# Order of products, buffers of raw strips and staging of gated blocks in a SwiGLU layer

## The chip, the cores and the metric

The kernel runs on one core of a Trainium2 chip. The metric is the device time of one execution in microseconds (us). The core's engines are TensorE (PE, matmuls), VectorE (DVE), ScalarE (ACT), GpSimd (POOL) and SyncE (SP); SP issues most DMA transfers, and each engine works through its own queue of instructions in order.

## What is computed

One decoder layer for a prompt of 1024 rows and 8 x 4 sample rows, 1056 columns T of activations in all. The change touches the last third of it, the SwiGLU feed-forward block:

```python
x = layer_norm(DEEPNORM_ALPHA * x + memory_attention(x, mem_k, mem_v, w_mem_q, w_mem_o), ln2_g, ln2_b)
ffn = (jax.nn.silu(x @ w_gate) * (x @ w_up)) @ w_down
x = layer_norm(DEEPNORM_ALPHA * x + ffn, ln3_g, ln3_b)
```

Here x has 1024 features and D_FF is 2816, which is NF = 22 strips of 128 hidden features. Inputs are float32.

## The kernel before

**Tiles.** The 1056 columns are three blocks, BLK: block 0 and block 1 of 384 columns, block 2 of 288. A float32 product is made of three reduced-precision (fp32r) matmuls: high times high, high times low, low times high (mm3, lines L209 to L211, and the function product). So each operand is first split: ScalarE casts the high part, VectorE subtracts it from the raw value and keeps the low part. Names that end in h or begin with whi are high parts; l and wlo mark low parts. (A weight unit of gate_up is one tile [128, 2, 512] with both parts, under the tag whi or wlo.)

**Stages.** gate_up_first makes strips f = 0 and 1 (NC = 2) with plain products (gemm). Its evacuation applies Silu on ScalarE (L948), multiplies on VectorE (L951) and writes the gated block sil to the DRAM scratch s_h (put, L938, on SP's queue). In the same stage combine makes the sums of activation blocks that gate_up needs: sums sq on GpSimd and VectorE (L973), casts (L979), low parts x1l, x6l, x7l on VectorE (L980).

gate_up makes f = 2 to 21. A pair f is a gate strip and an up strip of 1024 weights, four quarters a11, a12 (gate) and a21, a22 (up). Blocks 0 and 1 are computed by seven products instead of eight, as Strassen's scheme does: m4 and m3 use a22 and a11 alone, m2, m5, m1, m6, m7 use sums of quarters. Each is 12 matmuls of 384 columns. Block 2 takes four plain products (a11, a12, a21, a22), 48 matmuls of 288 columns, and these stand last in a pair. The nine units of a pair are made in the order of `names`: GpSimd sums quarters into wt (L1011, 3 buffers), ScalarE casts (L1013), VectorE subtracts (L1014). The code makes units four ahead of the product at hand; the scheduler then puts each engine's instructions in an order by its own planning, fixed when the kernel is built.

**Raw strips.** raw(f) loads the two strips of a pair on SP's queue (L994): the gate strip into tag wraw of the long-lived pool w, the up strip into tag wru of the pool up, two buffers each. The pool up (wru, wt and the products' staging) lies where the pool ln3 lay, which holds the sil and sq tiles of gate_up_first, so the first loads into wru and the first wt wait until those are done with.

**down** goes over the hidden strips in five groups (DOWN: 4, 4, 4, 2, 8 strips). For each block of a group it loads the gated strips from s_h, four at a time (hr, L1100), casts (L1103) and subtracts (L1104), and multiplies with the strips of w_down: each weight strip gives two outputs of four 128-row steps, block 0 for eight outputs, then block 1, then block 2. s_h is one DRAM tile, so a load from it waits for every write to it that stands earlier in the program.

Of the kernel before, what the change touches and what calls it, by code (L numbers as in the profile page):

```python
# [10 lines left out]
F32R = mybir.dt.float32r  # L11
# [11 lines left out]
NF = 22  # L23
# [117 lines left out]
class Body:  # L141
# [121 lines left out]
    def phase12(self, st):  # L263
# [13 lines left out]
        self.s_x1 = scr("s_x1", [128, 8 * T])  # L277
        self.s_h = scr("s_h", [128, NF * T])
        self.qs = self.t(self.cp, [128, 4, 32], "qs")
# [614 lines left out]
    def rest(self):  # L894
        tc, nc, a = self.tc, self.nc, self.a
        v, act, g, mm = nc.vector, nc.scalar, nc.gpsimd, nc.tensor.matmul
        x = self.x
        xs = lambda b, k: tuple(t_[:, k % 4, :] for t_ in x[b][k // 4])
        with tc.tile_pool(name="mq", bufs=1) as qp:
            self.mem_attention(qp, x, xs)  # L900
        with tc.tile_pool(name="z2", bufs=1) as zp:
            z = self.load_z(zp, self.s_x1)
            with tc.tile_pool(name="xc", bufs=1) as xp:
                with tc.tile_pool(name="ln3", bufs=1) as self.lp:
                    self.mem_out(z, xp, x, xs)
                    X = self.gate_up_first(z, xp, x, xs)
                with tc.tile_pool(name="up", bufs=1) as up:
                    self.gate_up(up, X, x[2])
            with tc.tile_pool(name="ln4", bufs=1) as self.lp, tc.tile_pool(name="ffn", bufs=1) as fp:
                self.down(z, fp)  # L910
# [25 lines left out]
    def put(self, t_, f, b):  # L936
        off, n = BLK[b]
        self.nc.sync.dma_start(self.s_h[:, NF * off + f * n:NF * off + (f + 1) * n], t_[:, :n])  # L938


    def gate_up_first(self, z, xp, x, xs):
        nc, sil, X = self.nc, {}, {}

        def evac(s, b, ps):
# [19 lines left out]
    def combine(self, X, xp, z, names):  # L964
# [5 lines left out]
        for n in names:  # L970
# [11 lines left out]
            yield  # L982

    def gate_up(self, up, X, x2):
        tc, nc, a = self.tc, self.nc, self.a
        v, act, g = nc.vector, nc.scalar, nc.gpsimd
        raws, units = {}, {}

        def raw(f):
            if f >= NF:  # L990
                return
            raws[f] = [self.t(self.wp, [128, 1024], "wraw", bufs=2), self.t(up, [128, 1024], "wru", bufs=2)]
            for i, r in enumerate(raws[f]):
                nc.sync.dma_start(r[:], a["wst"][GU + 2 * f + i])  # L994


        names = ("a22", "a11", "m2", "m5", "m1", "m6", "m7", "a12", "a21")

        def unit(i):
            f, n = NC + i // 9, names[i % 9]  # L1000
            if f >= NF:
                return
            if n == "a22":
                raw(f + 1)
            q = {f"a{1 + j // 2}{1 + j % 2}": raws[f][j // 2][:, 512 * (j % 2):512 * (j % 2) + 512] for j in range(4)}
            src = q.get(n)
            if src is None:
                p_, q_, op = {"m2": ("a21", "a22", OP.add), "m5": ("a11", "a12", OP.add), "m1": ("a11", "a22", OP.add),
                              "m6": ("a21", "a11", OP.subtract), "m7": ("a12", "a22", OP.subtract)}[n]
                src = self.t(up, [128, 512], "wt", bufs=3)[:]  # L1010
                g.tensor_tensor(out=src, in0=q[p_], in1=q[q_], op=op)  # L1011
# [14 lines left out]
        tt = v.tensor_tensor  # L1026
        raw(NC)
        for i in range(4):
            unit(i)
        at = 4  # L1030
        for f in range(NC, NF):
            U = lambda n: units[f, n]

            def step():
                nonlocal at
                unit(at)
                at += 1

            p4, p3 = self.ps(), self.ps()
            e4, e3, e1, d, s2 = (tmp(n, c) for n, c in (("e4", 1), ("e3", 2), ("e1", 2), ("ed", 1), ("s2", 2)))  # L1040
# [29 lines left out]
            step()  # L1070
            n = BLK[2][1]
            pg, pu = self.ps2(), self.ps2()
            product(pg, n, U("a11"), *x2[0])
            product(pg, n, U("a12"), *x2[1], first=False)
            sil = tmp("sil", 1)
            act.activation(sil[:, :n], pg[:, :n], AF.Silu)
            step()
            product(pu, n, U("a21"), *x2[0])
            product(pu, n, U("a22"), *x2[1], first=False)
            tt(out=sil[:, :n], in0=sil[:, :n], in1=pu[:, :n], op=OP.mult)  # L1080
            self.put(sil, f, 2)
            step()


    def down(self, z, fp):
# [3 lines left out]
        for ci, (f0, nf) in enumerate(DOWN):  # L1089
# [5 lines left out]
            for b, (off, n) in enumerate(BLK):  # L1095
                H[b] = []
                for k0 in range(0, nf, 4):
                    nk = min(4, nf - k0)
                    r = self.t(fp, [128, 4, 384], "hr")[:, :nk, :n]
                    nc.sync.dma_start(r, self.s_h[:, NF * off + (f0 + k0) * n:NF * off + (f0 + k0 + nk) * n]  # L1100
                                      .rearrange("p (k n) -> p k n", n=n))
                    h, l = (self.t(self.ap_, [128, 4, n], f"a{(ci + k0 // 4) % 2}{p}{b}", F32R)[:, :nk] for p in "hl")
                    nc.scalar.copy(h, r)  # L1103
                    nc.vector.tensor_tensor(out=l, in0=r, in1=h, op=OP.subtract)  # L1104
                    H[b].append((h, l))

# [401 lines left out]
```

## Time and profile before

| | us |
|---|---|
| runs | 1733.98, 1729.49, 1733.06 |
| median | 1733.06 |
| the profiled execution | 1729.63 |
| its span | 1727.8 |
| TensorE busy in the span | 1612.6 |
| VectorE, ScalarE, GpSimd busy | 937.8, 593.3, 553.3 |

The profile is that of one execution. The page gives busy time by engine and the chain of work that ended last; a chain row has a start, a length and what ran or was waited for. A table of windows gives, for a stretch, the busy time and number of instructions of each engine, the clock granted to TensorE as a share of 2.4 GHz, the busy share of the DMA engines and GB/s. A list of waits names the waiting engine and line, then what ended the wait, total us, times and longest us. A group of instructions has its count, busy time and mean ns, then the idle time ahead of it. gate_up_first ends at about 1004 us of the span, gate_up at 1436.4, down follows.

### The profile page before, as it was taken

How to read it: one execution, taken by the hardware profiler on the slowest of the kernel's cores; microseconds unless marked ns; L12 is line 12 of the kernel's file. 1: busy time of each engine (PE TensorE's matmuls, PEld its weight loads, DVE VectorE, ACT ScalarE, POOL GpSimd, SP SyncE). 2: the span in 40 equal slices, each digit the busy share in tenths (PEclk: the TensorE clock that was granted, in tenths of full speed). 3: DMA queues.
4: the chain of work that ended last, by engine and by line, in shares of the span. 5: the costliest groups of instructions: out<-in, count | busy, mean ns of one | idle time of the engine just before them, and what ended most of it. 6: DMA issues, size and time to landing. Idle time of an engine off the chain costs nothing.

```text
span 1727.8 us, 27767 instructions
## 1 busy us (share of the span) xinstructions
PE 1612.6 (93%) x10910; PEld 1472.8 (85%) x10910; DVE 937.8 (54%) x1754; ACT 593.3 (34%) x1149; POOL 553.3 (32%) x534
## 2 busy tenths in 40 slices
PE   7898898999999988999998979999999997999996
PEld 7787785666776978987798979999999997999995
DVE  7555482077545986235527765555555544544645
ACT  5211121186334255235404633333333332211312
POOL 3404402042222644002126555455554440000033
PEclk9998999999999998999999989999999998999998
DMA  7535776813422356126621212222222214422301
GB/s 271 119 67 144 203 202 174 273 67 126 139 70 85 127 196 223 49 84 213 243 74 46 67 66 75 78 75 78 75 75 75 75 62 142 141 83 68 113 38 64
DMA packets 103779, 200.71 MB, mean 116 GB/s; under 512 B 14240, under 2 KB 60832, under 8 KB 102880
## 3 DMA queue, kind: packets, MB, share of 16 engines
q1 hardware_dynamic: 90976, 152.79, 28.3%
q10 hardware_dynamic: 12672, 46.14, 8.0%
q8 instruction: 86, 1.41, 0.3%
q14 instruction: 45, 0.37, 0.1%
HBM read 153.85 MB, written 45.04 MB: 115 GB/s over the span
## 4 chain that ended last, share of the span: by engine, by line
PE 74%; DVE 11%; DMA 7%; ACT 2%; issue 2%; POOL 2%; SPq 1%; ACTq 0%; POOLq 0%; DVEq 0%
PE g L1021 16%; PE g L209 12%; PE g L211 12%; PE g L210 12%; PE s L1021 7%; PE s L575 2%; DMA wraw<-in_wst_dram 2%; PE s L577 2%; DVE wlo L191 1%; PE g L599 1%; DMA skv<-in_ckT_dram 1%; PE q L750 1%; POOL z L831 1%; DMA skv<-in_cv_dram 1%; PE g L411 1%
## 5 line engine op out<-in xcount | busy, mean ns | idle before, releaser
L209 PE MATMUL g<-a0h,whi 128*128 128x384 f32 (+1 forms) x768 | 255.9, 335 | 21.7 <-ACT a0h L1103 11.7
L211 PE MATMUL g<-a0h,wlo 128*128 128x384 f32 (+1 forms) x768 | 252.8, 329 | 5.0 <-DVE wlo L191 5.0
L210 PE MATMUL g<-a0l,whi 128*128 128x384 f32 (+1 forms) x768 | 253.9, 331 | 0.1
L209 PE MATMUL g<-a1h,whi 128*128 128x384 f32 (+1 forms) x672 | 221.4, 330 | 0.8 <-ACT a1h L335 0.8
L210 PE MATMUL g<-a1l,whi 128*128 128x384 f32 (+1 forms) x672 | 218.2, 325 | 2.9 <-DVE a1l L337 1.8
L211 PE MATMUL g<-a1h,wlo 128*128 128x384 f32 (+1 forms) x672 | 218.9, 326 | 0.0
L209 PEld LDWEIGHTS g<-a0h,whi 128*128 128x128 f32 x768 | 148.4, 194 | 27.8 <-ACT a0h L1103 12.0
L211 PEld LDWEIGHTS g<-a0h,wlo 128*128 128x128 f32 x768 | 148.7, 194 | 7.2 <-DVE wlo L191 5.7
L190 ACT CAST whi<-wraw 128x1024 fp32r<-128x1024 f32 x84 | 88.0, 1049 | 185.1 <-PE g L210 116.6
L210 PEld LDWEIGHTS g<-a0l,whi 128*128 128x128 f32 x768 | 148.9, 194 | 2.1 <-DVE a0l L1104 0.7
L191 DVE TENSOR_TENSOR wlo<-wraw,whi 128x1024 fp32r<-128x1024 f32 x84 | 113.3, 1352 | 68.2 <-ACT whi L190 67.9
L209 PEld LDWEIGHTS g<-a1h,whi 128*128 128x128 f32 x672 | 128.3, 191 | 6.0 <-issue 3.1
L210 PEld LDWEIGHTS g<-a1l,whi 128*128 128x128 f32 x672 | 128.2, 191 | 4.1 <-DVE a1l L337 2.0
L211 PEld LDWEIGHTS g<-a1h,wlo 128*128 128x128 f32 x672 | 128.0, 191 | 1.3 <-issue 1.1
L1011 POOL TENSOR_TENSOR wt<-wraw,wru 128x512 f32<-128x512 f32 x40 | 52.6, 1315 | 136.5 <-DVE wlo L1014 136.5
L776 DVE TENSOR_TENSOR z<-z,g 128x384 f32<-128x384 f32 (+1 forms) x96 | 49.1, 518 | 86.2 <-PE g L211 86.2
L1013 ACT CAST wlo<-wt 128x512 fp32r<-128x512 f32 x100 | 60.2, 618 | 83.4 <-PE g L1021 74.0
L1014 DVE TENSOR_TENSOR wlo<-wt,wlo 128x512 fp32r<-128x512 f32 x100 | 83.1, 846 | 3.0 <-ACT wlo L1013 1.4
L784 POOL TENSOR_TENSOR acc<-z 128x384 f32<-128x384 f32 (+1 forms) x6 | 8.0, 1339 | 205.4 <-DVE z L776 191.7
L1049 DVE TENSOR_TENSOR ed<-e,g 128x384 f32<-128x384 f32 x20 | 11.1, 554 | 105.9 <-PE g L1021 102.5
L831 POOL TENSOR_SCALAR z<-z,vneg,vecs 128x384 f32<-128x384 f32 (+1 forms) x36 | 50.5, 1414 | 43.6 <-DVE z L827 43.6
L587 POOL TENSOR_SCALAR S<-S,rD 128x128 f32<-128x128 f32 (+7 forms) x64 | 38.5, 607 | 68.7 <-DVE rD L586 49.8
(457 smaller groups left out, 4033.8 us busy)
## 6 DMA issues: line engine op xcount, KB each, us to landing
wraw<-in_wst_dram ACTq DMA_DIRECT2D x88, 512.0 KB, 3.9
skv<-in_ckT_dram SPq DMA_DIRECT2D x40, 256.0 KB, 4.6
skv<-in_cv_dram SPq DMA_DIRECT2D x40, 256.0 KB, 4.6
wraw<-in_wst_dram SPq DMA_DIRECT2D x20, 512.0 KB, 3.7
wru<-in_wst_dram SPq DMA_DIRECT2D x20, 512.0 KB, 4.4
kvm<-in_cmk_dram SPq DMA_DIRECT2D x16, 512.0 KB, 4.9
wraw<-in_cmv_dram SPq DMA_DIRECT2D x16, 512.0 KB, 4.1
hr<-s_h SPq DMA_DIRECT2D x10, 768.0 KB, 4.2
```

The costliest lines, as they stand in the source:

```text
L190: self.nc.scalar.copy(h[:], r[:])
L191: self.nc.vector.tensor_tensor(out=l[:], in0=r[:], in1=h[:], op=OP.subtract)
L209: mm(out, wh, xh, start=start, stop=False)
L210: mm(out, wh, xl, start=False, stop=False)
L211: mm(out, wl, xh, start=False, stop=stop)
L587: g.tensor_scalar(out=S[:, :w], in0=S[:, :w], scalar1=rD[:], scalar2=1.0, op0=OP.mult, op1=OP.mult)
L776: self.nc.vector.tensor_tensor(out=z[:, k], in0=z[:, k], in1=ps[:, :n], op=OP.add)
L831: g.tensor_scalar(out=z[:, k], in0=z[:, k], scalar1=sc, scalar2=bi, op0=OP.mult, op1=OP.add)
L1011: g.tensor_tensor(out=src, in0=q[p_], in1=q[q_], op=op)
L1013: act.copy(t_[:, 0], src)
L1014: v.tensor_tensor(out=t_[:, 1], in0=src, in1=t_[:, 0], op=OP.subtract)
L1021: nc.tensor.matmul(ps[:, :n], p_, q_, start=first and k + j == 0, stop=k == 3 and j == 2, skip_group_check=not first)
```

## The change

- raw(f) becomes a method; both strips of a pair go to one tag, wraw for even f, wru for odd f, two buffers each. raw(2) is called in gate_up_first, behind the write of strip 1's block 0, instead of at the start of gate_up; raw(f + 1) goes with the first unit of f.
- The four products of block 2 come first in each pair, and the units are made in the order a11, a12, a21, a22, m2, m5, m1, m6, m7. wt has two buffers.
- The scratch s_h becomes 33 tiles, one for two strips of one block.
- down loads two strips at a time into tiles of half the size. For the first group all six loads go through one tile hr0 that is allocated ahead of gate_up_first, for the others through two buffers.

```diff
-        self.s_h = scr("s_h", [128, NF * T])
+        self.s_h = {(f, b): scr(f"s_h{f}_{b}", [128, 2 * BLK[b][1]]) for f in range(NF // 2) for b in range(3)}
...
             z = self.load_z(zp, self.s_x1)
+            self.hr = self.t(zp, [128, 2, 384], "hr0")
...
     def put(self, t_, f, b):
-        off, n = BLK[b]
-        self.nc.sync.dma_start(self.s_h[:, NF * off + f * n:NF * off + (f + 1) * n], t_[:, :n])
+        n = BLK[b][1]
+        self.nc.sync.dma_start(self.s_h[f // 2, b][:, f % 2 * n:(f % 2 + 1) * n], t_[:, :n])
...
             self.put(sil[b], s // 2, b)
+            if s == 2 * NC - 1 and b == 0:
+                self.raw(NC)
...
+    def raw(self, f):
+        if f >= NF:
+            return
+        pool, tag = ((self.wp, "wraw"), (getattr(self, "up", None), "wru"))[(f - NC) % 2]
+        self.raws[f] = [self.t(pool, [128, 1024], tag, bufs=2) for _ in range(2)]
+        for i, r in enumerate(self.raws[f]):
+            self.nc.sync.dma_start(r[:], self.a["wst"][GU + 2 * f + i])
...
-        def raw(f):
-            if f >= NF:
-                return
-            raws[f] = [self.t(self.wp, [128, 1024], "wraw", bufs=2), self.t(up, [128, 1024], "wru", bufs=2)]
...
-        names = ("a22", "a11", "m2", "m5", "m1", "m6", "m7", "a12", "a21")
+        names = ("a11", "a12", "a21", "a22", "m2", "m5", "m1", "m6", "m7")
...
-            if n == "a22":
-                raw(f + 1)
+            if n == names[0]:
+                self.raw(f + 1)
...
-                src = self.t(up, [128, 512], "wt", bufs=3)[:]
+                src = self.t(up, [128, 512], "wt", bufs=2)[:]
...
-        raw(NC)
...
+            n = BLK[2][1]
+            pg, pu = self.ps2(), self.ps2()
+            product(pg, n, U("a11"), *x2[0])
+            product(pg, n, U("a12"), *x2[1], first=False)
...
+            product(pu, n, U("a21"), *x2[0])
+            product(pu, n, U("a22"), *x2[1], first=False)
...
-                for k0 in range(0, nf, 4):
-                    nk = min(4, nf - k0)
-                    r = self.t(fp, [128, 4, 384], "hr")[:, :nk, :n]
-                    nc.sync.dma_start(r, self.s_h[:, NF * off + (f0 + k0) * n:NF * off + (f0 + k0 + nk) * n]
-                                      .rearrange("p (k n) -> p k n", n=n))
...
+                for k in range(0, nf, 2):
+                    r = (self.hr if not ci else self.t(fp, [128, 2, 384], "hr", bufs=2))[:, :, :n]
+                    nc.sync.dma_start(r, self.s_h[(f0 + k) // 2, b][:].rearrange("p (k n) -> p k n", n=n))
```

**Entry of gate_up, SP's queue.** From the first raw load to the first load into wru, before (wraw_10114 and wru_10115 are the gate and up strip of f = 2, wraw_10118 and wru_10119 those of f = 3):

```order
L994 DMA wraw_10114<-in_wst_dram 128x1024
L994 DMA wraw_10118<-in_wst_dram 128x1024
L938 DMA s_h<-sil_9745 128x384
L938 DMA s_h<-sil_9828 128x384
L938 DMA s_h<-sil_9889 128x384
L938 DMA s_h<-sil_9943 128x384
L938 DMA s_h<-sil_10005 128x288
L938 DMA s_h<-sil_10077 128x288
L994 DMA wru_10115<-in_wst_dram 128x1024
L994 DMA wru_10119<-in_wst_dram 128x1024
```

And now (wraw_9897 and 9898 are both strips of f = 2, wru those of f = 3; s_h_0_97, s_h_1_98 and s_h_2_99 are blocks 0, 1, 2 of strips 0 and 1):

```order
L995 DMA wraw_9897<-in_wst_dram 128x1024
L995 DMA wraw_9898<-in_wst_dram 128x1024
L939 DMA s_h_0_97<-sil_9778 128x384
L939 DMA s_h_0_97<-sil_9861 128x384
L1104 DMA hr_1671_8946<-s_h_0_97 128x768
L939 DMA s_h_1_98<-sil_9926 128x384
L939 DMA s_h_1_98<-sil_9980 128x384
L939 DMA s_h_2_99<-sil_10042 128x288
L939 DMA s_h_2_99<-sil_10114 128x288
L995 DMA wru_10151<-in_wst_dram 128x1024
L995 DMA wru_10152<-in_wst_dram 128x1024
```

The second load ahead of the writes belongs to f = 2 instead of f = 3, both loads behind the last write belong to f = 3, and a load of hr0 stands behind the second write of block 0.

**Entry of gate_up, VectorE.** From the low part x1l to the first subtraction for a unit of gate_up, before (whi_10122 is a22 of f = 2):

```order
L980 TENSOR_TENSOR x1l_10014<-sq_10011,x1h_10013 128x1536
L951 TENSOR_TENSOR sil_10005<-sil_10005,g_10017 128x288
L980 TENSOR_TENSOR x6l_10047<-sq_10044,x6h_10046 128x1536
L980 TENSOR_TENSOR x7l_10080<-sq_10050,x7h_10079 128x1536
L951 TENSOR_TENSOR sil_10077<-sil_10077,g_10083 128x288
L1014 TENSOR_TENSOR whi_10122<-wru_10115,whi_10122 128x512
```

And now (whi_10155, wlo_10158, whi_10164, wlo_10161 are a11, a12, a22, a21 of f = 2):

```order
L984 TENSOR_TENSOR x1l_10051<-sq_10048,x1h_10050 128x1536
L1020 TENSOR_TENSOR whi_10155<-wraw_9897,whi_10155 128x512
L1020 TENSOR_TENSOR wlo_10158<-wraw_9897,wlo_10158 128x512
L953 TENSOR_TENSOR sil_10042<-sil_10042,g_10054 128x288
L984 TENSOR_TENSOR x6l_10084<-sq_10081,x6h_10083 128x1536
L1020 TENSOR_TENSOR whi_10164<-wraw_9898,whi_10164 128x512
L1020 TENSOR_TENSOR wlo_10161<-wraw_9898,wlo_10161 128x512
L984 TENSOR_TENSOR x7l_10117<-sq_10087,x7h_10116 128x1536
L953 TENSOR_TENSOR sil_10114<-sil_10114,g_10120 128x288
```

Four subtractions of f = 2 (L1020, L1014 before) stand ahead of the last product sil, where there was none.

**Entry of gate_up, TensorE.** The last matmuls of gate_up_first and what follows, before (g_10138 is m4, g_10139 m3 of f = 2, s_10277 the gate part of block 2):

```order
L209 MATMUL g_10083<-a1h_1754_9714,whi_9716 128x288
L210 MATMUL g_10083<-a1l_1755_9715,whi_9716 128x288
L211 MATMUL g_10083<-a1h_1754_9714,wlo_9717 128x288
L1021 MATMUL g_10138<-a1h_1783_10007,whi_10122 128x384
L1021 MATMUL g_10138<-a1l_1784_10008,whi_10122 128x384
L1021 MATMUL g_10139<-a0h_1778_9974,whi_10125 128x384
L1021 MATMUL g_10139<-a0l_1779_9975,whi_10125 128x384
L1021 MATMUL s_10277<-a0h_1752_9712,whi_10125 128x288
L1021 MATMUL s_10277<-a0l_1753_9713,whi_10125 128x288
L1021 MATMUL g_10138<-a1h_1783_10007,whi_10122 128x384 x2
```

Now the four products of block 2 and m4, m3 of f = 2 (s_10167, s_10168, g_10231, g_10232), 72 matmuls, stand behind L211 without a break; then come these (whi_10311 is a11 of f = 3; wlo_10253, wlo_10271, wlo_10197 are m1, m6, m2 of f = 2):

```order
L1027 MATMUL g_10232<-a0h_1781_10011,whi_10155 128x384
L1027 MATMUL s_10370<-a0h_1753_9745,whi_10311 128x288
L1027 MATMUL s_10370<-a0l_1754_9746,whi_10311 128x288
L1027 MATMUL s_10370<-a0h_1753_9745,whi_10311 128x288 x2
L1027 MATMUL g_10314<-x1h_10050,wlo_10253 128x384
L1027 MATMUL g_10314<-x1l_10051,wlo_10253 128x384
L1027 MATMUL s_10370<-a0l_1754_9746,whi_10311 128x288
L1027 MATMUL s_10370<-a0h_1753_9745,whi_10311 128x288 x2
L1027 MATMUL g_10315<-x6h_10083,wlo_10271 128x384
L1027 MATMUL g_10314<-x1h_10050,wlo_10253 128x384
L1027 MATMUL g_10231<-a0h_1698_9301,wlo_10197 128x384
L1027 MATMUL g_10231<-a0l_1699_9302,wlo_10197 128x384
```

Matmuls with a11 of f = 3, m1 and m6 now stand ahead of m2.

**End of gate_up, SP's queue.** The last writes to s_h and the first loads of hr, before:

```order
L938 DMA s_h<-e_2315_13795 128x384
L938 DMA s_h<-sil_13953 128x288
L938 DMA s_h<-s_2344_13997 128x384
L938 DMA s_h<-e_2341_13994 128x384
L938 DMA s_h<-sil_14146 128x288
L1100 DMA hr_14210<-s_h 128x1536
L1100 DMA hr_14216<-s_h 128x1536
L1100 DMA hr_14222<-s_h 128x4x288
```

And now (hr_1671 is the tile hr0; s_h_0_100 holds strips 2 and 3 of block 0, s_h_1_98 strips 0 and 1 of block 1):

```order
L939 DMA s_h_2_129<-sil_13847 128x288
L939 DMA s_h_1_128<-s_2324_13891 128x384
L939 DMA s_h_0_127<-e_2321_13888 128x384
L939 DMA s_h_2_129<-sil_14046 128x288
L1104 DMA hr_1671_8946<-s_h_0_100 128x768
L1104 DMA hr_1671_8946<-s_h_1_98 128x768
L939 DMA s_h_1_128<-s_2350_14090 128x384
L939 DMA s_h_0_127<-e_2347_14087 128x384
L1104 DMA hr_14627<-s_h_0_103 128x768
```

The load of strips 2 and 3 of block 0 stands ahead of the last two writes, and no load of a first-group tile names a tile that is written there.

## Rows read from the trace of the kernel before

**Rows 1.** The page: busy time of TensorE, and the chain that ended last, by engine.

```profile
PE 1612.6 (93%) x10910; PEld 1472.8 (85%) x10910; DVE 937.8 (54%) x1754; ACT 593.3 (34%) x1149; POOL 553.3 (32%) x534
...
PE 74%; DVE 11%; DMA 7%; ACT 2%; issue 2%; POOL 2%; SPq 1%; ACTq 0%; POOLq 0%; DVEq 0%
```

**Rows 2.** Windows of core 0: length, busy time (count) by engine, clock, DMA.

```profile
core 0: us, PE busy (x) PEld busy (x) DVE busy (x) ACT busy (x) POOL busy (x), PEclk, DMA share, GB/s
1022.20:1436.40 414.20, 414.11 (x2607) 414.05 (x2607) 214.38 (x296) 150.38 (x293) 207.97 (x156) 1.00 0.23 77
1004.10:1022.20 18.10, 7.56 (x35) 7.08 (x33) 11.74 (x11) 7.05 (x12) 6.82 (x5) 0.72 0.19 67
1436.40:1454.60 18.20, 6.33 (x20) 5.65 (x19) 4.33 (x5) 2.94 (x3) 0.00 (x0) 0.62 0.52 170
1460.00:1500.00 40.00, 40.00 (x255) 40.00 (x254) 21.15 (x28) 10.97 (x9) 0.00 (x0) 1.00 0.40 127
```

**Rows 3.** Chain of waits at the entry: start us, length us, what.

```profile
1000.26 0.36 DVE sil L951
1000.62 4.89 DVE x6l L980
...
1007.60 1.75 DMA s_h<-sil
...
1009.62 3.57 DMA wru<-in_wst_dram
...
1013.28 0.63 ACT whi L1013
```

**Rows 4.** Waits of 1000 to 1030; issues of line L994 in 940 to 1008.

```profile
PE g L1021 <- ACT whi L1013: 9.7, 1, 9.7
...
L994 SPq DMA_DIRECT2D wraw<-in_wst_dram x2: 333/333/333, 961.2 to 962.4; - x2
```

**Rows 5.** Windows, columns as in rows 2: clock around four idle stretches.

```profile
992.00:996.00 4.00, 3.05 (x24) 2.81 (x23) 4.00 (x3) 1.68 (x2) 2.30 (x2) 1.00 0.00 0
940.00:950.00 10.00, 4.78 (x22) 4.29 (x21) 8.39 (x6) 1.05 (x2) 7.27 (x4) 0.66 0.25 77
1012.00:1018.00 6.00, 4.04 (x14) 4.03 (x15) 4.07 (x3) 3.42 (x6) 4.48 (x3) 0.53 0.27 109
1448.00:1454.00 6.00, 5.55 (x16) 5.05 (x17) 1.76 (x1) 0.25 (x1) 0.00 (x0) 0.50 0.41 131
```

**Rows 6.** Chain of waits at the exit, and PE's wait in 1425 to 1470.

```profile
1437.22 4.86 DMA s_h<-sil
...
1442.27 4.33 DMA hr<-s_h
...
1446.77 1.48 ACT a0h L1103
...
1448.28 1.77 DVE a0l L1104
...
PE g L209 <- ACT a0h L1103: 11.7, 1, 11.7
```

**Rows 7.** Groups by form, 985 to 1022 (first), 1100 to 1400 (others).

```profile
L1014 DVE TENSOR_TENSOR whi<-wraw,whi 128x512 fp32r<-128x512 f32 x2 | 3.5, 1775 | 0.0
...
L1011 POOL TENSOR_TENSOR wt<-wraw,wru 128x512 f32<-128x512 f32 x29 | 37.5, 1294 | 106.8 <-DVE wlo L1014 106.8
...
L1014 DVE TENSOR_TENSOR whi<-wru,whi 128x512 fp32r<-128x512 f32 x14 | 9.7, 692 | 20.6 <-ACT whi L1013 20.6
```

**Rows 8.** The page: DMA issues, KB each, median us from issue to landing.

```profile
wraw<-in_wst_dram SPq DMA_DIRECT2D x20, 512.0 KB, 3.7
wru<-in_wst_dram SPq DMA_DIRECT2D x20, 512.0 KB, 4.4
```

**Rows 9.** Waits of 1022.2 to 1436.4: total us, times, longest.

```profile
POOL wt L1011 <- DVE wlo L1014: 147.8, 57, 4.5
...
ACT whi L1013 <- DMA wru<-in_wst_dram: 80.7, 18, 5.5
```

More of the change, by code (lines that the diff above doesn't have):

```diff
@@ L936, in put @@
     def put(self, t_, f, b):
-        off, n = BLK[b]
-        self.nc.sync.dma_start(self.s_h[:, NF * off + f * n:NF * off + (f + 1) * n], t_[:, :n])
+        n = BLK[b][1]
+        self.nc.sync.dma_start(self.s_h[f // 2, b][:, f % 2 * n:(f % 2 + 1) * n], t_[:, :n])
     def gate_up_first(self, z, xp, x, xs):
         nc, sil, X = self.nc, {}, {}
+        self.raws = {}
         def evac(s, b, ps):
@@ L986, in gate_up @@
         v, act, g = nc.vector, nc.scalar, nc.gpsimd
-        raws, units = {}, {}
-        def raw(f):
-            if f >= NF:
-                return
-            raws[f] = [self.t(self.wp, [128, 1024], "wraw", bufs=2), self.t(up, [128, 1024], "wru", bufs=2)]
-            for i, r in enumerate(raws[f]):
-                nc.sync.dma_start(r[:], a["wst"][GU + 2 * f + i])
-        names = ("a22", "a11", "m2", "m5", "m1", "m6", "m7", "a12", "a21")
+        raws, units = self.raws, {}
+        self.up = up
+        names = ("a11", "a12", "a21", "a22", "m2", "m5", "m1", "m6", "m7")
         def unit(i):
@@ L1037, in step @@
                 at += 1
+            n = BLK[2][1]
+            pg, pu = self.ps2(), self.ps2()
+            product(pg, n, U("a11"), *x2[0])
+            product(pg, n, U("a12"), *x2[1], first=False)
+            sil = tmp("sil", 1)
+            act.activation(sil[:, :n], pg[:, :n], AF.Silu)
+            step()
+            product(pu, n, U("a21"), *x2[0])
+            product(pu, n, U("a22"), *x2[1], first=False)
+            tt(out=sil[:, :n], in0=sil[:, :n], in1=pu[:, :n], op=OP.mult)
+            self.put(sil, f, 2)
+            step()
             p4, p3 = self.ps(), self.ps()
@@ L1070, in gate_up @@
             step()
[L1071 to L1082, printed above, removed]
     def down(self, z, fp):
@@ L1096, in down @@
                 H[b] = []
-                for k0 in range(0, nf, 4):
-                    nk = min(4, nf - k0)
-                    r = self.t(fp, [128, 4, 384], "hr")[:, :nk, :n]
-                    nc.sync.dma_start(r, self.s_h[:, NF * off + (f0 + k0) * n:NF * off + (f0 + k0 + nk) * n]
-                                      .rearrange("p (k n) -> p k n", n=n))
-                    h, l = (self.t(self.ap_, [128, 4, n], f"a{(ci + k0 // 4) % 2}{p}{b}", F32R)[:, :nk] for p in "hl")
+                for k in range(0, nf, 2):
+                    r = (self.hr if not ci else self.t(fp, [128, 2, 384], "hr", bufs=2))[:, :, :n]
+                    nc.sync.dma_start(r, self.s_h[(f0 + k) // 2, b][:].rearrange("p (k n) -> p k n", n=n))
+                    if k % 4 == 0:
+                        H[b].append([self.t(self.ap_, [128, 4, n], f"a{(ci + k // 4) % 2}{p}{b}", F32R) for p in "hl"])
+                    h, l = (t_[:, k % 4:k % 4 + 2] for t_ in H[b][k // 4])
                     nc.scalar.copy(h, r)
                     nc.vector.tensor_tensor(out=l, in0=r, in1=h, op=OP.subtract)
-                    H[b].append((h, l))
             def evac_d(n, b, ps):
```

## Prediction

> **What bounds the kernel now.** I read the page first: TensorE (PE) is busy for 93% of the span and has 74% of the chain that ended last [rows 1]. Only time in which PE stands, or runs at its low clock, can be won. The table of windows says where that is around the change [rows 2]. From 1022.2 to 1436.4 PE is busy 414.11 of 414.20 us: the loop over pairs f = 2 to 21 has nothing to give. Its 2607 matmuls make 0.1589 us each. A pair has 84 of 384 columns and 48 of 288: 132 x 0.1589 = 20.97 us, or 0.455 ns per column, so 2.10 us for a product of 384 columns and 1.57 us for one of 288 (estimates from that row).
>
> The two edges lose time. **Entry**, 1004.1 to 1022.2: 35 matmuls, worth 5.6 us, in 18.1 us, so 12.5 us lost. **Exit**, 1436.4 to 1454.6: 20 matmuls worth 3.5 us in 18.2, so 14.7 us lost. The ceiling is 27.2 us.
>
> At the entry the chain of waits [rows 3] goes from VectorE's x6l (4.89 us, stretched by GpSimd) over the last gated product sil, its write to s_h (1.75 us from 1007.60) and the load of wru (3.57 us) to a cast that ends at 1013.91 and lets PE start; PE waited 9.7 us for it. The other strips are no cause: the two loads of wraw went out at 961.2 and 962.4 [rows 4]. wru waited because its pool lies where the sil tiles lay. Until 1018 the granted clock is then 0.53, mostly the low level of 1.2 GHz [rows 5].
>
> At the exit the chain [rows 6] is the last write of s_h (4.86 us from 1437.22), the load of hr (4.33), cast (1.48) and subtraction (1.77). PE waits 11.7 us and then runs six microseconds at 0.50 [rows 5].
>
> **The change, part by part.** *Entry.* Both raw loads of f = 2 now go to wraw buffers and stand in SP's queue where the two wraw loads stood, ahead of all writes of sil; they land some 37 us before 1004. PE can go on there with f = 2: third block first (4 x 1.57 = 6.3 us), then m4 and m3 (4.2 us), 10.5 us of work in a stretch that was empty.
>
> VectorE feeds it. Its queue is now: x1l, subtractions for a11 and a12, sil, x6l, subtractions for a22 and a21, x7l, last sil. A subtraction takes 0.69 us alone, 1.78 beside GpSimd [rows 7]. x1l ends at 1000.26 [rows 3], so a11 and a12 are ready by 1003 to 1005, in time. x6l still ends near 1005.5, and a22 and a21 come 1.4 to 3.6 us later, at 1007 to 1009. PE wants a21 after two products, 1004.1 + 3.1 = 1007.2, and gets it near 1008.1: **0.9 us lost** (0 to 2).
>
> The old wait is not gone, it lies behind these products. Four subtractions delay the last sil by 2.8 to 7.1 us; I take 3.5, nearer the low end, since only the first pair meets GpSimd's sq. The write then lands near 1012.5 (before: 1009.35), and wt, the staging of GpSimd's sums, and wru, now both strips of f = 3, wait for it as before. PE ends m3 at 1004.1 + 0.9 + 10.5 = 1015.5. Its queue goes on with four matmuls of f = 3's a11, then m1 and m6, and only then the rest of m2. wru lands at 1012.6 + 3.6 = 1016.2; with the cast (0.63) PE has a11 at 1016.8. The sums for m1 and m6 come third and fourth on GpSimd (1.29 us each [rows 7], from 1012.5, with two wt buffers where there were three), and their casts stand behind f = 3's a22 on ScalarE: m6's first half near 1020.2, m1's second near 1020.9. PE has some ten matmuls (1.6 us) in 1015.5 to 1021.1: **4.0 us lost** (2 to 6).
>
> One pair later ScalarE and VectorE have f = 4's a11 ahead of f = 2's m7. f = 4's load can go only after GpSimd's sum for m7 of f = 2, near 1023, and lands 3.7 to 4.4 us later [rows 8]. PE wants m7 near 1029 and would stand **2.0 us** (0 to 4).
>
> The clock in 1015.5 to 1021: [rows 5] show it granted in full in 992 to 996 (PE busy 3.05 of 4 us) and 0.66 in 940 to 950 (4.78 of 10). My stretch looks more like the second. After 1013.9 it stayed low for some 4 us, which cost half of that. I take **1.0 us** (0 to 2.5). Entry after: 0.9 + 4.0 + 2.0 + 1.0 = 7.9 us lost; won 12.5 - 7.9 = **4.6 us**.
>
> *Loop.* Both strips of f + 2 are loaded when GpSimd's last sum of f has read the buffers of that parity, near 8.5 us after a pair's first product; they land by 12.2 and 14.0, then comes the cast, and behind it the copy e3 near 13.4 us. m5, which writes over what e3 copies, starts near 16.6 us. This cover of 3.2 us hides the load. ScalarE waits for wru in each pair already, 80.7 us in 18 waits [rows 9], with PE full. Casts, subtractions, sums and matmuls are as many as before; of wt's two buffers for three I expect longer waits of GpSimd, which has 57 of them with PE full [rows 9]. **0 us**, from 0 to the price of the slower rival below; a gain is excluded, since PE has none to give.
>
> *Exit.* The scratch is 33 tiles now, so a load waits only for the two pairs that it reads. The first half of block 0 goes to hr0 during the entry, 400 us early; on SP its wait for the second write of its tile delays later writes by under 2 us (1.75 each), and the next sil comes later than that: 0. Its cast goes to the a0 tile that m2 of f = 21 reads last, that is after m2: m5, m6, m7 and the rest of m1 follow, 6.4 us before the end. Half of 1.48 and half of 1.77 us, some waiting for VectorE: hr0 is read about 4.1 us before the end. Then the second half is loaded, 3.5 to 4.3 us (by [rows 6, 8], where a 768 KB hr takes 4.33 and 512 KB take 3.7 at least), cast and subtracted: high part 0.2 to 1.0 us after the last gate/up matmul, low part 1.1 to 1.9. PE wants the high part after six matmuls (1.0 us) and the low part after 14 (2.4): **0.5 us** (0 to 2). Block 1's second half is third through hr0, ready 16 to 19 us after the end, wanted after eight outputs, about 17: **0.5 us** (0 to 2). The 15 additional casts, subtractions and loads are of half size, and in 1460 to 1500 ScalarE was busy 11 and VectorE 21 of 40 us [rows 2]: 0. Exit: 14.7 - 1.0 = **13.7 us won**, the low clock with it, since PE no longer stands.
>
> **Sum:** 4.6 + 13.7 = 18.3 us. The profiled execution took 1729.63 (span 1727.8 and 1.8 around it): 1711.3. The median of the runs shown is 1733.06: 1714.8. They lie at both ends of the runs, so I count from the middle, 1731.3: **1713.0**.
>
> **Rivals.** *The entry's gain is given back.* The waits behind m3 are longer than reckoned (GpSimd stretches all four subtractions, the clock stays low), and 12.5 us are lost again, only later: 1731.3 - 13.7 = 1717.6. For it: wru and wt still hang on the last sil. Against: 10.5 us of products stand ahead of it. 0.15. The Trainium skill, "TensorE: Matmul & The Clock Gate", section "A second HAM failure mode: psum-queue depth-cycling", says that short idle times between groups of matmuls can send the clock gate back and forth, and that throughput is lost between the bursts; by that rule this rival would be likelier than I make it, and [rows 5] bear it out in one of two stretches.
>
> *Both edges nearly free.* Only 0.9 us lost at the entry and 0.5 at the exit: 1731.3 - 25.8 = 1705.5. It needs m1 and m6 in time, against the queue order. 0.12.
>
> *The halves queue behind hr0.* If the second half of block 0 starts only when PE is at the end, PE waits a load, cast and subtraction (4.2 + 0.75 + 0.9 = 5.9 us), and the low clock costs 2 more: the exit wins 6.8, all 11.4: 1719.9. It decides if hr0 is read after m6 rather than ahead of it. 0.10. The Trainium skill, "DMA: Bandwidth & Descriptors", section "Rules for kernel authors", would rather have small transfers made into one; [rows 6, 8] agree in so far as 512 KB land hardly sooner than 768.
>
> *Slower: the loop stalls in each pair.* The cast of f + 2's a11 heads ScalarE's queue, ahead of the copy e3 and of m7's cast. If its load lands more than 3.2 us later than I count, PE stops at m5 in 18 pairs. From 1.3 us each (23.4 us, as much as 18.3 + 5.2) the kernel is slower; at 2 us it is 1713 + 36 = 1749. Against: loads land in about 4 us now. 0.05. A milder form, 0.2 to 0.7 us each, gives 1717 to 1726: 0.05.
>
> *It doesn't do what it says:* a wait that I overlooked holds f = 2's or hr0's data, both edges stay, 1729 to 1734. 0.04.
>
> **How the numbers follow.** The forecast (entry losing 5 to 10 us, exit 0 to 3) has 0.49 and by itself 1709 to 1718. Down to 1704 the range takes in the free edges, up to 1722 the entry's gain given back, the halves and part of the mild stall; under 2 in 10 are left out. About 0.3%, 5.2 us, is what a measurement of this kernel can tell from no change. Faster by more: 0.88; within: 0.06 (no effect, the end of the mild stall); slower: 0.06.
>
> **What would show it.** Right: matmuls of line L1027 go on within 0.3 us of 1004.1; a thin stretch near 1015 to 1021, ended by casts and subtractions of m1 and m6; a wait of 0 to 4 us near 1030; 20.9 to 21.0 us per pair; at the exit L209 follows the last L1027 within 1 us at clock 1.00. Wrong: a wait of PE in every pair, a clock of 0.5 behind the exit, or PE waiting over 2 us for the cast of hr.

## The result

| | before | changed |
|---|---|---|
| runs | 4, 1728.91 to 1733.98 | 4, 1707.12 to 1716.61 |
| median, us | 1731.28 | 1708.87 |
| profiled execution, us | 1729.63 | 1716.61 |
| ratio | | 0.9879, 95% interval 0.9844 to 0.9914 |

The kernel before has one run more here than above. The changed kernel is faster by 22.4 us at the median. The forecast was 1713.0, range 1704 to 1722.

The profiled execution of the changed kernel happens to be its longest. In the rows that answer to [rows 1], the page says that TensorE's share went from 93% to 94%:

```profile
PE 1611.6 (94%) x10910; PEld 1471.4 (86%) x10910; DVE 935.5 (55%) x1769; ACT 598.8 (35%) x1164; POOL 541.2 (32%) x534
...
PE 72%; DVE 11%; DMA 8%; ACT 3%; issue 2%; POOL 2%; SPq 1%; ACTq 0%; POOLq 0%; DVEq 0%
```

To see the change alone, the span is cut at the two edges of gate_up. This is the timeline of TensorE in the changed kernel (start us, length us, instruction) where gate_up_first ends:

```profile
1013.01 0.29 PE L211 MATMUL g<-a1h,wlo 128*128 128x288 f32 x1
1013.14 0.30 PE L1027 MATMUL s<-a0h,whi 128*128 128x288 f32 x1
```

And the same view where gate_up ends:

```profile
1437.53 0.33 PE L1027 MATMUL g<-x7h,wlo 128*128 128x384 f32 x1
1437.70 0.33 PE L209 MATMUL g<-a0h,whi 128*128 128x384 f32 x1
```

At both edges the next matmul follows at once, 0.13 and 0.17 us later, where PE waited 9.7 and 11.7 us before [rows 4, 6]. The last plain matmul starts at 1013.01 here and started at 1003.99 before: 9 us were lost in stages that the change doesn't touch. Behind that point the same windows of both kernels (columns as in [rows 2]) show what the change gave. Before:

```profile
1004.10:1436.40 432.30, 421.67 (x2642) 421.13 (x2640) 226.12 (x305) 157.43 (x305) 214.79 (x160) 0.99 0.23 76
1436.40:1727.80 291.40, 264.44 (x1606) 259.77 (x1604) 143.48 (x204) 63.14 (x63) 34.16 (x26) 0.95 0.28 91
```

And after, with the entry in three pieces:

```profile
1013.10:1437.60 424.50, 422.19 (x2642) 420.71 (x2641) 221.40 (x304) 159.33 (x301) 201.15 (x160) 1.00 0.23 77
1013.10:1024.00 10.90, 10.59 (x73) 10.35 (x72) 6.75 (x8) 3.02 (x5) 2.67 (x3) 1.00 0.25 80
1024.00:1031.00 7.00, 5.11 (x21) 4.36 (x20) 5.56 (x7) 3.56 (x7) 4.75 (x4) 0.76 0.23 90
1031.00:1040.00 9.00, 8.90 (x53) 8.40 (x52) 4.69 (x7) 4.18 (x8) 4.83 (x4) 1.00 0.36 119
1437.60:1714.80 277.20, 261.54 (x1606) 257.15 (x1604) 145.39 (x220) 65.41 (x79) 36.26 (x27) 0.97 0.29 95
```

The same 2642 recorded matmuls take 424.5 us instead of 432.3, and the same 1606 behind them 277.2 instead of 291.4. That is 7.8 us at the entry and 14.2 us at the exit, 22.0 in all, as the medians say. The forecast had 4.6 and 13.7.

What is left at the entry: PE works through 73 matmuls without a gap worth the name (10.59 of 10.9 us), then comes a thin stretch of 7 us with 21 matmuls at clock 0.76, then work is dense again. PE's waits from 990 to 1460 us (total, times, longest), those of gate_up:

```profile
PE s L1027 <- DVE whi L1020: 1.1, 1, 1.1
...
PE s L1027 <- ACT whi L1019: 0.8, 1, 0.8
PE s L1027 <- DVE wlo L1020: 0.3, 1, 0.3
```

The first two are waits for a11 of f = 3 in the thin stretch, the third is the wait for a21 of f = 2. The chain of waits (start, length) tells why the stretch is there:

```profile
1017.03 1.67 DVE x7l L984
1018.70 0.37 DVE sil L953
...
1019.09 1.73 DMA s_h<-sil
...
1021.24 2.54 POOL wt L1017 x2
```

x7l, the last sil, its write, and only then GpSimd's first sums: this is the old wait, with the last sil 5.7 us after the entry. At the exit the chain (start, length) is:

```profile
1432.16 0.74 ACT a0h L1108
...
1432.93 0.97 DVE a0l L1109
...
1433.91 3.02 DMA hr<-s_h
...
1436.96 0.51 ACT a0h L1108
```

The first half of block 0 is cast and subtracted and hr0 read by 1433.9, 3.8 us before the end of gate_up; the second half has landed at 1436.9 and its cast runs while gate_up still does.

### The profile page after: what moved, and what is told of

It reads as the page before. It is cut to its first block, busy times and chain, and to the rows that moved or that the text cites. A ratio compares the mean times of both kernels' runs of the same rounds, so it can differ in the third digit from the quotient of the medians.

```text
span 1714.8 us, 27782 instructions
## 1 busy us (share of the span) xinstructions
PE 1611.6 (94%) x10910; PEld 1471.4 (86%) x10910; DVE 935.5 (55%) x1769; ACT 598.8 (35%) x1164; POOL 541.2 (32%) x534
## 4 chain that ended last, share of the span: by engine, by line
PE 72%; DVE 11%; DMA 8%; ACT 3%; issue 2%; POOL 2%; SPq 1%; ACTq 0%; POOLq 0%; DVEq 0%
PE g L1027 16%; PE g L209 11%; PE g L211 11%; PE g L210 11%; PE s L1027 7%; DMA wraw<-in_wst_dram 2%; PE s L575 2%; PE s L577 2%; PE g L599 1%; DVE wlo L191 1%; PE q L750 1%; DMA hr<-s_h 1%; POOL z L831 1%; DMA skv<-in_cv_dram 1%; DMA skv<-in_ckT_dram 1%
## 5 line engine op out<-in xcount | busy, mean ns | idle before, releaser
L211 PE MATMUL g<-a0h,wlo 128*128 128x384 f32 (+1 forms) x768 | 253.3, 330 | 4.0 <-DVE wlo L191 4.0
L211 PE MATMUL g<-a1h,wlo 128*128 128x384 f32 (+1 forms) x672 | 218.2, 325 | 0.0
L211 PEld LDWEIGHTS g<-a0h,wlo 128*128 128x128 f32 x768 | 149.1, 194 | 6.2 <-DVE wlo L191 4.8
L211 PEld LDWEIGHTS g<-a1h,wlo 128*128 128x128 f32 x672 | 127.5, 190 | 1.3 <-issue 1.1
L1020 DVE TENSOR_TENSOR wlo<-wt,wlo 128x512 fp32r<-128x512 f32 x100 | 91.5, 915 | 26.5 <-ACT wlo L1019 24.7
L1195 POOL TENSOR_SCALAR S<-S,rD 128x256 f32<-128x256 f32 x32 | 15.2, 478 | 116.2 <-DVE rD L1184 110.5
L1017 POOL TENSOR_TENSOR wt<-wraw,wraw 128x512 f32<-128x512 f32 x30 | 39.4, 1314 | 22.1 <-DVE wlo L1020 22.1
```

Of the source, the lines that this page charges most:

```text
L211: mm(out, wl, xh, start=False, stop=stop)
L1020: v.tensor_tensor(out=t_[:, 1], in0=src, in1=t_[:, 0], op=OP.subtract)
```

## The experiments

Each kernel's profile was cut in the same way. "gate_up" is the time from the last plain matmul's start to the last gate_up matmul's start, "rest" from there to the end of the span, "a pair" the time between the a21 products of successive pairs in the loop, all read from the timelines. These lengths are steadier than the totals: in the profiles of all kernels gate_up starts anywhere from 1000.3 to 1013.0 us, after stages that none of them changes.

| kernel | gate_up | rest | a pair | median of the runs |
|---|---|---|---|---|
| before | 432.3 | 291.5 | 20.974 | 1731.28 |
| the change | 424.5 | 277.3 | 20.974 | 1708.87 |
| change_again | 424.8 | 278.3 | 20.974 | 1708.89 |
| entry_only | 425.1 | 294.4 | 20.974 | 1724.07 |
| exit_only | 432.6 | 278.7 | 20.974 | 1715.79 |
| third_last | 424.6 | 277.8 | 20.974 | 1708.56 |
| one_scratch | 424.8 | 277.0 | 20.974 | 1706.02 (one run) |
| no_hr0_wt3 | 426.0 | 292.3 | 20.974 | 1720.34 (one run) |
| sil_apart | 423.8 | 277.8 | 21.054 | 1707.83 |
| sil_pad | 423.2 | 276.5 | 20.973 | 1705.86 |
| third_last_pad | 423.1 | 278.0 | 20.974 | 1706.21 |
| shift_128 | 426.2 | 279.0 | 21.054 | 1710.76 (one run) |
| shift_384 | 426.2 | 276.9 | 21.054 | 1709.99 (one run) |

Twenty pairs of 20.974 us are 419.5 us, so what a kernel loses at the entry is its gate_up less 419.5: 12.8 us before, 5.0 and 5.3 in the two profiles of the change. "rest" of kernels with the same exit differs by up to 2.5 us.

**The change once more (change_again).** No edit.

> The changed kernel once more, unaltered. In its first profile the last plain matmul of gate_up_first stood at 1013.0 us of the span, 9 us later than in the kernel before, after stages that the change does not touch, and that execution took 1716.6 us where three others took 1707 to 1710. Theory: this lateness belongs to that one execution, not to the change; here gate_up starts near 1004 to 1006 and the execution takes 1707 to 1710. Rival: the change itself delays the earlier stages (it asks for its first strips earlier), then gate_up starts near 1013 in this profile too. In both, from that start the stretch to the last gate_up matmul takes 424 to 425 us (432.3 before) and the rest 277 us (291.4 before).

It starts gate_up at 1005.2 us, and the median of five runs is 1708.89 (ratio 0.9864, 0.9841 to 0.9886). So the 9 us in the first profile are that execution's, and the lengths behind the start repeat to 0.3 and 1.0 us.

**Each edge alone.** entry_only takes the exit's part out of the change:

```diff
-        self.s_h = {(f, b): scr(f"s_h{f}_{b}", [128, 2 * BLK[b][1]]) for f in range(NF // 2) for b in range(3)}
+        self.s_h = scr("s_h", [128, NF * T])
...
-            self.hr = self.t(zp, [128, 2, 384], "hr0")
...
-                for k in range(0, nf, 2):
-                    r = (self.hr if not ci else self.t(fp, [128, 2, 384], "hr", bufs=2))[:, :, :n]
+                for k0 in range(0, nf, 4):
+                    nk = min(4, nf - k0)
+                    r = self.t(fp, [128, 4, 384], "hr")[:, :nk, :n]
...
```

> The change without its part at the exit: one scratch tile, and hr loaded four strips at a time from the pool of down, as before. Theory (the two edges are independent; the exit is worth 14): gate_up 424 to 425 us as in the change, and behind its last matmul a wait of 11 to 13 us for the cast of hr and then the low clock, so the rest takes 291 to 293 us; total 1722 to 1725. Rival (the new order of products gives part of the exit, since block 2 is written earlier): the rest takes 284 to 288 us, total 1715 to 1719.

exit_only is the kernel before with the exit's part and the smaller wt:

```diff
-        self.s_h = scr("s_h", [128, NF * T])
+        self.s_h = {(f, b): scr(f"s_h{f}_{b}", [128, 2 * BLK[b][1]]) for f in range(NF // 2) for b in range(3)}
...
+            self.hr = self.t(zp, [128, 2, 384], "hr0")
...
-                src = self.t(up, [128, 512], "wt", bufs=3)[:]
+                src = self.t(up, [128, 512], "wt", bufs=2)[:]
...
+                for k in range(0, nf, 2):
+                    r = (self.hr if not ci else self.t(fp, [128, 2, 384], "hr", bufs=2))[:, :, :n]
...
```

> The kernel before with 33 scratch tiles, halves of hr, the tile hr0, and two wt buffers instead of three (three would not fit beside hr0); strips and order of products as before. Theory: entry as before (gate_up 432 us), the rest 277 to 278 us as in the change, total 1716 to 1718. Rival (two wt buffers cost something in the old order, where the sums come earlier in a pair): waits of PE in the pairs, gate_up over 435 us, total 1720 or more.

PE's wait at the exit of entry_only (total, times, longest):

```profile
PE g L209 <- ACT a0h L1107: 14.4, 1, 14.4
```

And at the entry of exit_only, 9.7 us as in [rows 4]:

```profile
PE g L1022 <- ACT whi L1014: 9.7, 1, 9.7
```

The theory holds in both: the edges are independent, gate_up is 425.1 and 432.6, rest 294.4 and 278.7. Three sizes lie a little outside what was expected: in entry_only the rest (291 to 293) and the wait (11 to 13), in exit_only the rest (277 to 278). The order of products gives nothing to the exit (294.4 is not less than 291.5): the last write went out 4.3 us behind the last matmul of gate_up, where it was 0.9 before, since it now ends a longer row of steps behind m7. Two wt buffers cost nothing in the old order: the pair is 20.974.

**Which part of the entry? (third_last)** The products of block 2 and the units go back to the old order, the early loads stay:

```diff
-        names = ("a11", "a12", "a21", "a22", "m2", "m5", "m1", "m6", "m7")
+        names = ("a22", "a11", "m2", "m5", "m1", "m6", "m7", "a12", "a21")
...
-            n = BLK[2][1]
-            pg, pu = self.ps2(), self.ps2()
...
             self.put(e3, f, 0)
             step()
+            n = BLK[2][1]
+            pg, pu = self.ps2(), self.ps2()
...
```

> The change with the products of block 2 last in each pair and the units in the order of before (a22, a11, m2, m5, m1, m6, m7, a12, a21); early loads, alternating buffers, scratch tiles and hr0 as in the change. Theory (the products of block 2 cover the latency of the first sums): PE goes on with m4, m3 and one product of block 2, some 5.8 us, then stands 4 to 5 us for m2, and the low clock follows, so gate_up takes 427 to 429 us, the rest 277 to 279; total 1711 to 1714. Rival (only the early loads count): gate_up 424 to 425 us, total 1708 to 1710.

The theory falls. gate_up is 424.6 us, as with block 2 first. PE does less before it must wait, and waits for m2 alone, for its cast and then for its subtraction (waits of PE in third_last):

```profile
PE g L1027 <- ACT wlo L1019: 2.5, 1, 2.5
...
PE g L1027 <- DVE wlo L1020: 0.5, 1, 0.5
```

The stretch of that wait, as a window, is as thin and at as low a clock as the one in the change:

```profile
1012.00:1020.00 8.00, 4.95 (x20) 4.40 (x19) 4.11 (x4) 3.76 (x7) 7.00 (x5) 0.79 0.41 135
```

A likely reason, not tested apart: only two subtractions stand ahead of the last sil in VectorE's queue instead of four, and the products of block 2 that were not done in the gap cover later waits. From exit_only, whose order of products is the same, third_last differs by the early, alternating loads alone: 432.6 to 424.6. With them, the order of products adds nothing; the new order without them was not run.

**Which part of the exit? (one_scratch, no_hr0_wt3)** One scratch tile, the rest as in the change:

```diff
-        self.s_h = {(f, b): scr(f"s_h{f}_{b}", [128, 2 * BLK[b][1]]) for f in range(NF // 2) for b in range(3)}
+        self.s_h = scr("s_h", [128, NF * T])
...
```

> The change with one scratch tile in place of 33; halves and hr0 stay. The prediction said that a load of hr waits only for what it reads because the scratch is 33 tiles. Theory by that step: with one tile the first load waits for the last write again, PE stands 9 to 12 us behind gate_up, the rest takes 291 to 294 us. Rival (the loads waited in the kernel before because hr's buffer lies where the staging tiles of gate_up lay, and had to wait until the last of those was written out; writes to other parts of one scratch tile hold nobody): the rest takes 277 to 279 us as in the change.

And the opposite, 33 scratch tiles without hr0:

```diff
-            self.hr = self.t(zp, [128, 2, 384], "hr0")
...
-                src = self.t(up, [128, 512], "wt", bufs=2)[:]
+                src = self.t(up, [128, 512], "wt", bufs=3)[:]
...
-                    r = (self.hr if not ci else self.t(fp, [128, 2, 384], "hr", bufs=2))[:, :, :n]
+                    r = self.t(fp, [128, 2, 384], "hr", bufs=2)[:, :, :n]
```

> The change without hr0: the halves of the first group go through the pool of down like the others; the space goes to a third wt buffer. Scratch in 33 tiles. Theory of the scratch: loads wait only for what they read, so PE waits for one load, cast and subtraction, 5 us, and the low clock: rest 283 to 286 us. Theory of the buffer's place: the loads wait for the last write out of the staging tiles, PE waits 10 to 12 us, the rest takes 290 to 294 us. Entry: if the second wt buffer was what m1 and m6 waited for, gate_up takes 423 to 424 us; if not, 424.5 to 425.

PE's one wait behind gate_up in one_scratch:

```profile
PE g L209 <- DVE z L774: 0.3, 1, 0.3
```

In no_hr0_wt3 PE's wait is:

```profile
PE g L209 <- ACT a0h L1107: 12.5, 1, 12.5
```

And the chain to it (start us, length us, what):

```profile
1430.46 1.88 DMA s_h<-e
...
1432.59 5.44 DMA hr<-s_h
...
1438.20 0.84 ACT a0h L1107
...
1439.06 0.97 DVE a0l L1108
```

With one scratch tile and hr0 the rest takes 277.0 us; with 33 tiles and no hr0 it takes 292.3, PE waits 12.5 us, and the load of hr again follows the last write, although it reads strips written 400 us earlier. Each is one run, but the 15 us between them are far more than the 2.5 us by which kernels with the same exit differ. So writes to other parts of one scratch tile hold nobody, and the sentence under "The kernel before" that a load from s_h waits for every earlier write to it is wrong: as built, the loads of one_scratch carry the same waits as those of the change. What held the load was the memory of its pool: the pool of down lies over the place of gate_up's pools, and its first load carries waits for the last writes out of the staging tiles. The bytes of hr itself lie where x6l and x7h lay, not where a staging tile lay. So the wait belongs to the pool as a whole, and SP's queue has the load behind those writes. The tile hr0, allocated ahead, is the exit's gain; the division of the scratch is not, and neither are the halves by themselves (292.3 is not less than 291.5). The third wt buffer gives nothing at the entry either: gate_up takes 426.0 us, 1 us above the 424.5 to 425 expected for that case, and why it is more stays open.

**The thin stretch at the entry (sil_apart, sil_pad, third_last_pad).** The last sil is moved out of the pool whose place wt and wru take:

```diff
+            self.zp = zp
...
-                sil[b] = self.t(self.lp, [128, 384], "sil", bufs=2)
+                sil[b] = self.t(self.zp, [128, 288], "sil0") if b == 2 else self.t(self.lp, [128, 384], "sil", bufs=2)
...
-            sil = tmp("sil", 1)
+            sil = self.t(up, [128, 288], "sil")[:]
```

> The change, with the gated block 2 of strips 0 and 1 kept in a tile of its own outside the pool whose place wt and wru take over. The first wt and wru then wait for the low part x7l instead of the last write of the scratch, some 2 us earlier. Theory (the wait for that write, and the load of f = 3 behind it, is what leaves the thin stretch of 3.7 us at 1024 to 1031 in the change): the stretch loses 1 to 2 us instead of 3.7, gate_up takes 422 to 423 us instead of 424.5, total 1706 to 1707.5. Rival (the sums, casts and subtractions for m1 and m6 are what PE waits for, whatever releases them): 424 to 425 us, total as the change, 1708 to 1709.

gate_up takes 423.8 us, between theory and rival. At the entry the theory is right: its loss is 423.8 - 20 x 21.054 = 2.7 us where the change has 5.0 to 5.3, and the granted clock stays at 1.00. But each pair takes 0.080 us more, 1.6 us in the loop. sil_pad changes the width of that tile alone:

```diff
-                sil[b] = self.t(self.zp, [128, 288], "sil0") if b == 2 else self.t(self.lp, [128, 384], "sil", bufs=2)
+                sil[b] = self.t(self.zp, [128, 320], "sil0") if b == 2 else self.t(self.lp, [128, 384], "sil", bufs=2)
```

> As sil_apart, but the separate tile is 320 columns wide instead of 288. In sil_apart the entry lost 2 us less than in the change, yet each pair of the loop took 21.054 us where it takes 20.974 in the kernel before, in the change and in the two half changes; the matmuls that read x1, x6 and x7 have means of 337 to 339 ns there, 334 and 339 in the change, with the same order of matmuls. Those six tiles lie behind the separate tile: their start in a partition is a multiple of 512 bytes in sil_apart, 384 past one before and in the change, 128 past one here. Theory (the place of a moving tile in its partition sets that): a pair takes 20.97 us again, gate_up 422 to 422.5 us, total 1705 to 1707. Rival (the separate tile itself, or the freed wait, slows the loop): 21.05 us per pair, gate_up 423.8 us, total as sil_apart.

The pair is back at 20.973, and the median of five runs, 1705.86, is the lowest of all (ratio to the kernel before 0.9853, 0.9831 to 0.9875; the interval overlaps that of the change, so only the 1.3 to 1.6 us in gate_up speak for it). gate_up is at 423.2, 0.7 us above the 422.5 expected at most: the entry loses 3.7 us, 1 us more than in sil_apart, and 0.5 us of that is a wait for the copy e3, one pair later. What PE waits for at the entry now, beside a21, is m1 on ScalarE and VectorE: it was second in line behind that write, by the mechanism of sil_apart's rival (waits of PE in sil_pad):

```profile
PE g L1028 <- DVE wlo L1021: 0.9, 1, 0.9
PE g L1028 <- ACT wlo L1020: 0.8, 1, 0.8
```

And its entry as a window, 23.64 of 25.6 us busy at clock 1.00 throughout:

```profile
1004.40:1030.00 25.60, 23.64 (x147) 22.54 (x146) 16.61 (x20) 10.76 (x19) 11.21 (x10) 1.00 0.30 100
```

third_last_pad puts the same tile into third_last.

> Block 2 last in each pair, as in third_last, with the separate tile of sil_pad (320 columns). third_last took 424.6 us in gate_up as the change does, with one wait of 2.5 us for m2's cast; sil_pad took 423.2. Theory (whatever the order, PE waits for the first sums, and these for the last reader of the place that wt takes over): without the last write in front of the sums m2 comes 2 us earlier, one wait of 0.5 to 1 us is left, gate_up takes 421.5 to 423 us, total 1703 to 1706, at or a little under sil_pad. Rival (block 2 first has its worth once the write is gone): 424 us and more, total 1707 to 1709.

gate_up takes 423.1 us and the median is 1706.21. Both lie just above the theory's ranges and below the rival's: the gain over third_last is 1.5 us where 1.6 to 3.1 were expected. The longest wait that is left is 1.2 us for the cast of m1, not of m2. Order of products and wait are independent here too.

**The place of the moving tiles (shift_128, shift_384).** The change, with unused bytes behind hr0, here 32 columns (shift_384: 96):

```diff
-            self.hr = self.t(zp, [128, 2, 384], "hr0")
+            self.hr = self.t(zp, [128, 800], "hr0")[:, :768].rearrange("p (k n) -> p k n", n=384)
```

> The change with 128 unused bytes per partition behind hr0: the order of matmuls is the same, x1, x6 and x7 start at a multiple of 512 bytes in their partition, as in sil_apart, instead of 384 past one. Theory (the start of the moving tiles sets the pace): a pair takes 21.05 us instead of 20.97, gate_up 426 to 426.5 us. Rival (the slow pairs of sil_apart came from something else that the separate tile changed): 20.97 us per pair.

> As shift_128 with 384 unused bytes: the six tiles start 256 past a multiple of 512 bytes. If the pace falls with starts that are multiples of 256, a pair takes 21.05 us; if only multiples of 512 are slow, 20.97.

Both take 21.054 us per pair. These are groups of matmuls from 1100 to 1400 us (count, busy us, mean ns), those that read x1h and x7l in change_again first:

```profile
L1027 PE MATMUL g<-x1h,wlo 128*128 128x384 f32 x117 | 32.0, 334 | 0.0
...
L1027 PE MATMUL g<-x7l,wlo 128*128 128x384 f32 x56 | 19.0, 339 | 0.0
```

x1h in shift_384:

```profile
L1027 PE MATMUL g<-x1h,wlo 128*128 128x384 f32 x113 | 31.5, 339 | 0.0
```

x1h in sil_apart:

```profile
L1028 PE MATMUL g<-x1h,wlo 128*128 128x384 f32 x119 | 33.0, 339 | 0.0
```

x1h in sil_pad:

```profile
L1028 PE MATMUL g<-x1h,wlo 128*128 128x384 f32 x119 | 32.5, 334 | 0.0
```

The matmuls of m1 and m6 (x1, x6) have means of 337 to 339 ns where the six tiles start at a multiple of 256 bytes in their partition (sil_apart and both shifts), 334 where they start 128 past one (the change, sil_pad). Those of m7 (x7) have 337 to 339 in all of these kernels, though their tiles start where the others do. The order of matmuls is the same in the change and the shifts.

The two shifts also show what the fall of the clock in the thin stretch is worth. This is that stretch in shift_128 (columns as in [rows 2]):

```profile
1014.70:1021.70 7.00, 5.11 (x21) 4.37 (x20) 5.59 (x7) 3.59 (x7) 4.72 (x4) 0.76 0.23 90
```

And in shift_384:

```profile
1016.10:1023.10 7.00, 4.81 (x24) 3.53 (x23) 5.55 (x7) 3.55 (x7) 4.76 (x4) 1.00 0.24 93
```

The clock fell in the one and not in the other, and gate_up takes 426.2 us in both. In one_scratch, too, it stayed at 1.00, and the entry lost 5.3 us. Where it stayed, PE then stood for the cast of m6 as well (0.5 us in one_scratch).

## Why the prediction was right, and where it was not

**What bounds the kernel:** right. Only the two edges changed, and the loop cost exactly nothing: 20.974 us per pair in both kernels, against 20.97 worked out from the count of matmuls. The rival of the stalling loop had no part in it.

**The entry,** 4.6 us forecast, 7.8 measured; lost 7.9 forecast, 5.0 to 5.3 measured. Its terms, each measured from start to start of the matmuls in the first profile:

- a21: 0.9 forecast, 0.6 measured (0.3 of it listed as a wait).
- The thin stretch: 4.0 of waits and 1.0 of clock forecast, 3.9 measured for both (7 us with 21 matmuls worth 3.3 us). It began 10.9 us after the entry, where 11.4 was worked out. The term that was wrong is the clock's: it did fall (0.76 over the stretch, 1.00 behind it), but shift_384 and one_scratch lose as much without the fall, so it is not to be added to the waits. The recorded waits in the change are 1.9 us for a11 of f = 3. m1 and m6, which the forecast had last, came in time there, at the low clock; at the full one m6 holds PE, and with the write out of the way m1 does (sil_apart, sil_pad).
- The last sil, on which the stretch hangs: a delay of 3.5 forecast, 2.5 measured (its write starts 6.1 us after the entry, 3.6 before). The subtraction for a12 took 3.98 us beside GpSimd's sum, but x6l, now behind it, 1.74 where it took 4.99.
- One pair later: 2.0 forecast, 0.6 measured, just ahead of m7. f = 4's load went out 18 us after the entry (19 forecast), so the error is in what PE still had to do ahead of m7: it started m7 26.6 us after the entry, where 24.9 was reckoned.
- The premise that block 2's products, put first, fill the empty stretch is true of what PE did, but not the reason of the gain: third_last has the same gate_up without it. What makes up for it there is argued above, not shown.

**The exit,** 13.7 us forecast, 14.2 measured. The sizes hold: hr0 was read 3.8 us before the end (4.1 forecast), the second half came in time, block 1's second half cost 0.6 us at most (49.39 of 50 us busy from 1450 to 1500). One step failed, the reason given: "The scratch is 33 tiles now, so a load waits only for the two pairs that it reads." The chain in [rows 6] shows the last write ahead of the load, and I read it as a wait for data. It was a wait for the memory of the pool, and one_scratch and no_hr0_wt3 show it: 277.0 and 292.3. By its own reason the forecast of the exit came out by luck, because hr0 stood beside the scratch in the same change.

**The rivals.** The halves did not queue up behind hr0 (block 0's second half landed at 1436.94, 0.8 us before gate_up's end). The entry's gain was not given back, though the old wait and the low clock were both there. The rule of the Trainium skill ("TensorE: Matmul & The Clock Gate", section "A second HAM failure mode: psum-queue depth-cycling") is borne out in part: in the thin stretch the clock fell once in the change (0.76 over 7 us) and not at all in shift_384, and the fall took no throughput, as gate_up is 426.2 us in both shifts. For the rule of the Trainium skill in "DMA: Bandwidth & Descriptors", section "Rules for kernel authors", the page of the changed kernel's profile shows the price (KB each, median us to landing):

```profile
hr<-s_h SPq DMA_DIRECT2D x22, 384.0 KB, 3.4
```

Half the size takes 3.4 us, where a whole one took 4.33 [rows 6]. Two halves thus cost more than one whole, as the rule has it, but none of it was on the path.

**The total:** 1708.87 against 1713.0; of 4.1 us, 3.2 are the entry's and 0.5 the exit's, and the rest lies within the scatter of the stages ahead. A single total depends most on when gate_up starts: 1000.3 to 1013.0 us over all profiles.

## What to carry to other kernels

Cut the span at the stages that a change touches and compare the lengths of the pieces; here they repeat to about a microsecond while totals scatter by ten. When a chain shows a transfer behind a write, ask whether it waits for the data or for the memory that its pool inherits: an early, long-lived buffer of 3 KB per partition took away 14 us, and a strip that no longer went to an inherited place took away 8. And before crediting an order of work with a gain, undo the order alone. The same holds for the clock: a kernel with the same order whose clock did not fall showed that the fall had cost nothing.

## What the runs showed of the hardware

The start of a matmul's moving tile within its partition can matter a little: a pair took 0.080 us more when the moving tiles of m1, m6 and m7 started at a multiple of 256 bytes, where the stationary tiles and all other moving tiles start 128 past one. Starts of 0 and 256 past a multiple of 512 were both slow, 128 and 384 both fast. Nearly all of it is in the 24 matmuls of m1 and m6 (means of 337 to 339 ns against 334). The 12 of m7 had 337 to 339 ns at every start, so the start alone does not set the pace, and what holds m7 stays open. Whether the start itself counts or its place relative to the stationary tiles was not tried.

A fall of the granted clock to 0.76 over 7 us, with PE waiting for other engines in the same stretch, cost nothing here: shift_128 had it, shift_384 had 1.00, and gate_up took 426.2 us in both (one run each).
